# Four edits to a two-block transformer kernel: consumers of GpSimd powers, 128-row gate products, moved weights, an earlier final norm

## The chip, the cores and the metric

The kernel runs on one core of a Trainium2 chip, in one launch. Its time is the device time of that core in microseconds (us). Before the change the median of three runs is 1242.46 us (1242.16 to 1245.07). The profile is one further execution of 1242.75 us.

The engines are TensorE (PE in the profile; its weight loads are PEld), VectorE (DVE), ScalarE (ACT), GpSimd (POOL) and SyncE (SP), which issues most of the weight DMAs. Each engine works through its own queue in order, and waits there until what its next instruction reads is ready.

## The reference

Two transformer blocks follow each other on 512 tokens of width 1024, in fp32. Cut to what the change touches:

```python
# block 1
xn = rmsnorm(h, norm_mix_g)
q, k, v, u_vg, f = split(xn @ w_in)                 # 8 heads of 64
c = cumsum(log_sigmoid(f + b_forget))               # the gates, one column a head
att = softmax(causal(q @ k.T * scale + c_q - c_k)) @ v
u, vg = split(gelu(u_vg))
vg = rmsnorm(vg by groups of 64, v_gain)
h += concat(att, u * (tril(w_s) @ vg + b_s)) @ w_out
h += (silu(g) * a) @ w_down                         # a, g: conv3(rmsnorm(h) @ w_up)
x = rmsnorm(h, norm_final_g)
# block 2
h = modulate(rmsnorm(x), ...);  lat, krope, ca = split(h @ w_in_2)
o_ca  = chunk_attention(rmsnorm(ca_q), rmsnorm(ca_k), ca_v)      # 8 heads
o_mla = mla_attention(rope(rmsnorm(lat @ w_q_up)), ...)          # 8 heads
x += g_a * (concat(o_mla, o_ca) @ w_out_2)
x += g_m * ((silu(gate) * val) @ w_down_2)
```

## The kernel before

Activations lie in 128-partition tiles over the 512 tokens. An fp32 product is done as three products of rounded parts, high x high, high x low and low x high (`mm` in `gemm_fm`, `gemm_part`, `gemm_tm`, all recorded at L369). A weight piece arrives by DMA as `wraw`, ScalarE rounds it to `whi` (L347) and VectorE or GpSimd takes the rest as `wlo` (L348). Pieces are loaded ahead in the order of `make_plan`; the fourth entry of a plan item is a skew, in elements, of `whi` and `wlo` within their tiles of 1088 elements. Where `halves` is set a product runs over 256 tokens and then over the other 256: the first up tiles of the two FFNs, the last down tile, the latents, and the last parts of the attention outputs.

TensorE's order is the order of the code, written by hand. The orders of VectorE, ScalarE and GpSimd come from a scheduler that goes by readiness and priorities: `AHEAD` pulls the preparation of a head forward, `BEHIND` pushes background jobs back. A `Fill` is a list of generators that are run bit by bit between attention strips: `fill` holds products for TensorE, `bg` holds VectorE and GpSimd jobs such as normalisations and rope.

A strip is 128 queries of one head. `strip_scores` makes its scores on TensorE and the running minimum on VectorE (L590; the scores are negated), after which ScalarE makes the exponentials `p` (L594). One strip later `strip_turn` transposes `p` on TensorE (L603) and copies it to `pt` (L605), and after a further strip `strip_values` multiplies by the values into `o`. Block 1 has 32 strips, block 2 has 64; (h, q) is strip q of head h.

Inverse square roots are powers on GpSimd (L523) of a small tile: `ss` for the gated half of block 1 (used by VectorE at L1104 on `uv`), `ssc` for the queries and keys of the chunk attention (L1423 on `ca`), `nw` for the latent queries (L1514 on `mqk`). In block 1, `cumulate` puts the cumulated gates as high and low rows into `cum` (64 rows, L1213 and L1214), and for each head one product with a column of `pick` spreads them over 128 partitions (`mm<-cum,pick`); `ch` and `cm` are copied from it for the strip minima. The final norm of block 1 is `final`: a power, then per half of the tokens four products of `ms` with the identity (`to_rows`) and eight VectorE instructions on `x` (L912). Only the residual of block 2's output needs its result. It was put into `bg` when `mla(1)`, the second group of latent heads, was begun.

Of the kernel before, what the change touches and what calls it, by code (L numbers as in the profile page):

```python
# [2 lines left out]

# [7 lines left out]
F32 = mybir.dt.float32  # L11
# [222 lines left out]
class Kernel:  # L234
# [41 lines left out]
    def make_plan(self):  # L276
        i, plan = self.i, []

        def fm(name, tiles, kt0=0, nk=KT, pool=False, last=None):
            for n in tiles:  # L280
                for p in self.fm_pieces(i[name], n, kt0, nk):
                    plan.append((p, pool, None, 0))
            if last:
                plan[-1] = plan[-1][:2] + (last, 0)

        def tm(name, n, nk=KT, pool=True, last=None, per=None):
            skew = SKEW // 4 if n < 384 else 0
            for p in self.tm_pieces(i[name], n, nk, per):
                plan.append((p, pool, None, skew))
            if last:  # L290
                plan[-1] = plan[-1][:2] + (last, 0)

        def parts(name, dest):
            for p in range(4):
                for g in range(2):
                    plan.append((i[name][p, g], False, dest.get((p, g)), 0))

        def ffn(up, down, last=None):
            for j in range(NF):
                fm(up, [j, j + NF])  # L300
            fm(down, range(KT), 0, NF, last=last)

        tm("w_v", 512, pool=False, per=1)
        tm("w_g1", 264, pool=False)
        fm("w_qk", [0, 4])
        fm("w_qk", [1, 5])
        tm("w_g0", 256, pool=False)
        tm("w_u", 512)
        fm("w_qk", [2, 6], pool=True)
        fm("w_qk", [3, 7], pool=True)  # L310

        parts("w_out", {(3, 1): ("mx", "mix", "mix")})
        ffn("w_up", "w_down", ("cv", "cv", "cv"))
        fm("w_lat", range(3))
        tm("w_ck0", 256, pool=False, last=("one", "m0", "m1"))
        tm("w_cq0", 288, pool=False)
        tm("w_cv0", 256, pool=False)
# [12 lines left out]
        ffn("w_up_2", "w_down_2")  # L330
        self.plan, self.loaded, self.taken = plan, [], 0
        self.ada_left, self.pools, self.before = [], {}, []

    def load_split(self, src, pool, dest, skew):

# [179 lines left out]
    def rsqrt(self, x):  # L515
# [6 lines left out]
            e = e.rearrange("p (a b c) -> p a b c", b=shape[1], c=shape[2])  # L522
        self.nc.gpsimd.tensor_tensor(out=x, in0=x, in1=e, op=ALU.pow)  # L523

    def rstd(self, ms, scale, bias):

        r = self.sm.tile([P, 2], F32, tag="rstd", name="rstd", bufs=4)
        self.nc.vector.tensor_scalar(out=r, in0=ms, scalar1=scale, scalar2=bias, op0=ALU.mult, op1=ALU.add)
        self.rsqrt(r)
        return r  # L530
# [47 lines left out]
    def strip_scores(self, hd, qi):  # L578

        nc = self.nc  # L580
        nk = (qi + 1) * P
        n = max(nk, 256)
        s = self.bank("s")
        qk = hd["qk"]
        for j, (q, k) in enumerate(qk):
            self.mm(s[:, :n], q[:, qi * P:(qi + 1) * P], k[:, :n], j == 0, j == len(qk) - 1)
        st = self.sm.tile([P, 2], F32, tag="st", name="st", bufs=4)
        parts = hd["bias"](qi)
        for j, (cs, b) in enumerate(parts):
            nc.vector.tensor_tensor_reduce(  # L590
                out=s[:, cs], in0=s[:, cs], in1=b, scale=1.0, scalar=3e38 if j == 0 else st[:, j - 1:j],
                op0=ALU.add, op1=ALU.min, accum_out=st[:, j:j + 1])
# [410 lines left out]
    def block1_mix(self, xn, x, evac, evac_last, norm_a):  # L1003
# [24 lines left out]
        la = one.tile([P, 4, 8], F32, name="la")  # L1028


        cum = one.tile([64, 512], F32R, name="cum")
        pick = one.tile([64, 8], F32R, name="pick")
        nc.vector.tensor_tensor(out=pick, in0=self.ident[0:64, 0:8], in1=self.ident[0:64, 32:40], op=ALU.add)
        ss = one.tile([P, 2, 4, 4], F32, name="ss")


# [50 lines left out]
        def gate(j):  # L1087

            vs = [uv[t][:, 512 + 256 * j:768 + 256 * j] for t in range(4)]
            for t, v in enumerate(vs):  # L1090
                gelu2(v)
                sq = self.pp.tile([P, 512], F32, tag="p", name="sqg")[:, :256]
                nc.gpsimd.tensor_tensor(out=sq, in0=v, in1=v, op=ALU.mult)
                nc.vector.tensor_reduce(out=ss[:, j, t], in_=sq.rearrange("p (g d) -> p g d", d=64),
                                        axis=AX.X, op=ALU.add)
                yield 1200

            nc.vector.tensor_scalar(out=ss[:, j], in0=ss[:, j], scalar1=1.0 / 64, scalar2=4 * EPS,
                                    op0=ALU.mult, op1=ALU.add)
            self.rsqrt(ss[:, j])  # L1100
            yield 1500
            for t, v in enumerate(vs):
                v3 = v.rearrange("p (g d) -> p g d", d=64)
                nc.vector.tensor_tensor(out=v3, in0=v3, op=ALU.mult,  # L1104
                                        in1=ss[:, j, t].unsqueeze(2).to_broadcast([P, 4, 64]))
                nc.gpsimd.tensor_tensor(out=v, in0=v, in1=gg_row[:, 256 * j:256 * j + 256], op=ALU.mult)
                yield 700

# [36 lines left out]
        def qk(pr):  # L1145
            def ev(n, ps, cs):
                with self.tc.high_priority(offset=AHEAD):
                    if n < 4:
                        qf[pr] = two.tile([P, 512], F32, tag="qf", name="qf")
                        nc.vector.scalar_tensor_tensor(out=qf[pr], in0=ps, scalar=-0.125, in1=rrow,  # L1150
                                                       op0=ALU.mult, op1=ALU.mult)
                    else:
                        kf[pr] = two.tile([P, 512], F32, tag="kf", name="kf")
                        nc.vector.tensor_tensor(out=kf[pr], in0=ps, in1=rrow, op=ALU.mult)
            return self.gemm_fm(i["w_qk"], [pr, 4 + pr], xn, ev)

        def tm(w, dst):
# [48 lines left out]
        def cumulate():  # L1206

            cp = self.bank()[0:64]
            for t in range(4):
                for j, l in enumerate((lfh, lfl)):  # L1210
                    self.mm(cp[:, t * P:], l[:, t], tri[:, :512 - t * P], t == 0 and j == 0, t == 3 and j == 1)
            with self.tc.high_priority(offset=AHEAD):
                nc.scalar.copy(cum, cp)  # L1213
# [21 lines left out]
        def head(h):  # L1235
# [5 lines left out]
            def prepare(h):  # L1241
# [2 lines left out]
                qs = self.stack(stk, qf[pr], kf[pr], odd)  # L1244

                cp = self.bank()
                self.mm(cp, pick[:, h:h + 1].to_broadcast([64, P]), cum, True, True)
                ch = two.tile([P, 512], F32, tag="ch", name="ch")
                cm = two.tile([P, 512], F32, tag="cm", name="cm")
                nc.any.tensor_copy(out=ch, in_=cp)  # L1250
# [77 lines left out]

    def block2_mix(self, xn, norm_b, final, evac, evac_last, norm_a):
        nc, i = self.nc, self.i  # L1330
        ctx = ExitStack()
        self.pt = self.pool("pt2", 3, ctx=ctx)
        self.pp = self.pool("pp2", 3, ctx=ctx)
# [73 lines left out]
        def ca_norm(z, j):  # L1407
# [12 lines left out]
            yield 1500  # L1420
            for t in range(4):
                v3 = ca_slice(t, z, j).rearrange("p (g d) -> p g d", d=64)
                nc.vector.tensor_tensor(out=v3, in0=v3, op=ALU.mult,  # L1423
                                        in1=ss[:, j, z, t].unsqueeze(2).to_broadcast([P, 4, 64]))
                yield 400

        def cq0_evac(t, ps):
# [27 lines left out]
        def cq0():  # L1455
            yield from self.gemm_tm(i["w_cq0"], 288, xn, cq0_evac)
            bg.add("w_cq0", ca_norm(0, 0))
            bg.add("rope", rope())

        bg = Fill()  # L1460
        f = Fill([
# [42 lines left out]
        def q_norm(c):  # L1504
# [6 lines left out]
            for a in range(2):  # L1511
                v = mq[c][a]
                rq = r[:, 2 * a:2 * a + 2].unsqueeze(3)
                nc.vector.tensor_tensor(out=v, in0=v, in1=rq.to_broadcast([P, 2, 4, QK]), op=ALU.mult)  # L1514
# [34 lines left out]
        def mla(c):  # L1549
            if c == 0:  # L1550
                bg.add("kr", kr_rope())
            else:
                bg.add("final", final)
            mq[c] = m_tiles(0, c)
            yield from self.gemm_tm(i[f"w_q{c}"], 384, [lath[0], lath[1]], q_evac(c))
            bg.add(f"mq{c}", q_norm(c))
# [138 lines left out]
```

## Time and profile before

| | before |
|---|---|
| median of 3 runs | 1242.46 us |
| profiled execution | 1242.75 us |
| its span on the core | 1240.9 us |
| TensorE busy | 1206.9 us (97%) |
| VectorE busy | 792.5 us (64%) |
| ScalarE busy | 539.2 us (43%) |
| GpSimd busy | 194.2 us (16%) |
| mean granted clock of TensorE | 0.989 |

Of the 40 slices of the page, all but four have TensorE at 9 tenths or more; these four have 8, and three of them lie between 650 and 810 us, in the attention of block 2 (the fourth is the last). A busy TensorE may still run at half its clock or at a wider spacing than it could, so the start times of its products are read beside its busy time. In the timeline, what stands in brackets behind an instruction is how long its engine had been idle before it, and whose end released it.

### The profile page before, as it was taken

What the parts mean: (1) busy time and instruction counts of PE and PEld (TensorE: products, weight loads), DVE (VectorE), ACT (ScalarE), POOL (GpSimd) and SP (SyncE); (2) the same over time, 40 slices, a digit from 0 to 9 for tenths busy, and PEclk for the clock granted to TensorE, in tenths of its full rate; (3) what the DMA queues carried; (4) which work ended last, traced back from release to release, by engine and by line L of the source; (5) the groups of instructions that cost most, each with busy time, mean ns of one, the idle gap of its engine ahead of it and who ended that gap; (6) DMA issues with size and microseconds to landing.
All of it is one profiled execution on the core that took longest, in us unless ns stands there. A gap on an engine that the chain in (4) does not pass through costs nothing.

```text
span 1240.9 us, 17330 instructions
## 1 busy us (share of the span) xinstructions
PE 1206.9 (97%) x6730; PEld 1049.5 (85%) x6730; DVE 792.5 (64%) x1415; ACT 539.2 (43%) x963; POOL 194.2 (16%) x208
## 2 busy tenths in 40 slices
PE   9999999999999999999998998899999999999998
PEld 6887878988888888888998897789988888888887
DVE  6555877688888886433666779766676566553221
ACT  6444544444444443223435555664554444442110
POOL 1457400300000000000344452501200000000000
PEclk9999999999999999999999999999999999999999
DMA  7321212156666656433122111110132222233330
GB/s 242 99 86 48 73 68 69 52 190 200 189 202 195 193 185 193 129 94 114 56 103 64 56 69 61 51 35 18 69 119 87 101 102 92 96 94 103 117 110 17
DMA packets 40033, 131.57 MB, mean 106 GB/s; under 512 B 4608, under 2 KB 5504, under 8 KB 39952
## 3 DMA queue, kind: packets, MB, share of 16 engines
q1 hardware_dynamic: 31536, 102.64, 25.2%
q10 hardware_dynamic: 8208, 27.27, 7.1%
q8 instruction: 52, 0.85, 0.3%
q0 software_dynamic: 208, 0.57, 0.2%
q14 instruction: 29, 0.24, 0.1%
HBM read 128.37 MB, written 2.10 MB: 105 GB/s over the span
## 4 chain that ended last, share of the span: by engine, by line
PE 85%; DVE 7%; POOL 4%; ACT 2%; issue 2%; DMA 1%; SPq 0%; POOLq 0%; ACTq 0%; DVEq 0%
PE mm L369 74%; PE s L369 4%; PE o L369 3%; PE s L603 2%; DVE wlo L348 1%; DVE nt L550 1%; DMA x<-in_xT_dram 1%; DVE ca L1423 1%; DVE s L590 0%; POOL ss L523 0%; POOL nw L523 0%; PE s L695 0%; DVE kl L669 0%; DMA cs<-in_c_dram 0%; PE mm L1635 0%
## 5 line engine op out<-in xcount | busy, mean ns | idle before, releaser
L348 DVE TENSOR_TENSOR wlo<-wraw,whi 128x1024 fp32r<-128x1024 f32 (+4 forms) x182 | 210.4, 1158 | 182.0 <-ACT whi L347 181.2
L347 ACT CAST whi<-wraw 128x1024 fp32r<-128x1024 f32 (+4 forms) x194 | 192.2, 994 | 281.3 <-PE mm L369 261.8
L369 PE MATMUL mm<-xnh,whi 128*128 128x512 f32 (+1 forms) x832 | 312.4, 375 | 1.1 <-DVE nt L550 0.6
L369 PE MATMUL mm<-xnl,whi 128*128 128x512 f32 (+1 forms) x832 | 311.0, 374 | 0.0
L369 PE MATMUL mm<-xnh,wlo 128*128 128x512 f32 (+1 forms) x832 | 310.7, 373 | 0.0
L369 PEld LDWEIGHTS mm<-xnh,whi 128*128 128x128 f32 x832 | 157.0, 189 | 28.7 <-PE mm L369 0.8
L369 PEld LDWEIGHTS mm<-xnh,wlo 128*128 128x128 f32 x832 | 157.1, 189 | 27.7
L369 PEld LDWEIGHTS mm<-xnl,whi 128*128 128x128 f32 x832 | 157.2, 189 | 27.1
L369 PE MATMUL mm<-gh,whi 128*128 128x512 f32 (+1 forms) x384 | 141.6, 369 | 1.1 <-DVE x L937 0.6
L369 PE MATMUL mm<-gl,whi 128*128 128x512 f32 (+1 forms) x384 | 141.3, 368 | 0.0
L369 PE MATMUL mm<-gh,wlo 128*128 128x512 f32 (+1 forms) x384 | 141.3, 368 | 0.0
L729 DVE SCALAR_TENSOR_TENSOR cv<-mm,cols,cv 128x510 f32<-128x510 f32 (+1 forms) x176 | 130.4, 746 | 2.6 <-ACT cv L727 0.6
L369 PE MATMUL mm<-whi,xnh 128*128 128x256 f32 (+3 forms) x304 | 97.7, 321 | 0.2 <-ACT xnh L812 0.2
L369 PE MATMUL mm<-wlo,xnh 128*128 128x256 f32 (+3 forms) x304 | 94.3, 310 | 0.2 <-DVE wlo L348 0.2
L369 PE MATMUL mm<-whi,xnl 128*128 128x256 f32 (+3 forms) x304 | 94.2, 310 | 0.1
L369 PEld LDWEIGHTS mm<-gh,whi 128*128 128x128 f32 x384 | 72.4, 188 | 13.6 <-DVE x L937 0.8
L369 PEld LDWEIGHTS mm<-gl,whi 128*128 128x128 f32 x384 | 72.4, 188 | 12.1
L369 PEld LDWEIGHTS mm<-gh,wlo 128*128 128x128 f32 x384 | 72.4, 188 | 12.0
L594 ACT ACTIVATE p<-s,st 128x128 f32<-128x128 f32 (+1 forms) x96 | 50.7, 528 | 69.7 <-DVE st L590 66.7
L998 DVE CUSTOM_DVE_ANT_0 wada<-wada,cs,cols 128x1024 f32<-128x1024 f32 x48 | 61.5, 1282 | 26.9 <-DMA wada<-in_w_ada_dram 26.7
L369 PE MATMUL mm<-mix,whi 128*128 128x256 f32 (+1 forms) x288 | 74.4, 346 | 2.7 <-ACT vm L1563 1.2
L727 ACT ACTIVATE cv<-mm,cols 128x512 f32<-128x512 f32 x88 | 67.6, 772 | 0.2 <-PE mm L369 0.2
(293 smaller groups left out, 1839.1 us busy)
## 6 DMA issues: line engine op xcount, KB each, us to landing
wraw<-in_w_up_dram SPq DMA_DIRECT2D x88, 512.0 KB, 3.4
wada<-in_w_ada_dram ACTq DMA_DIRECT2D x48, 512.0 KB, 3.6
wraw<-in_w_down_dram SPq DMA_DIRECT2D x32, 512.0 KB, 3.5
wraw<-in_w_out_dram SPq DMA_DIRECT2D x16, 512.0 KB, 3.4
wraw<-in_w_down_dram SPq DMA_DIRECT2D x16, 384.0 KB, 3.1
wraw<-in_w_qk_dram SPq DMA_DIRECT2D x8, 512.0 KB, 3.7
wraw<-in_w_v_dram SPq DMA_DIRECT2D x8, 256.0 KB, 4.9
x<-in_xT_dram SPq DMA_DIRECT2D x8, 256.0 KB, 6.4
```

What stands on the lines that cost most here:

```text
L347: nc.scalar.copy(hi[:, :n], raw[:, :n])
L348: (nc.gpsimd if pool else nc.vector).tensor_tensor(out=lo[:, :n], in0=raw[:, :n], in1=hi[:, :n].bitcast(F32), op=ALU.subtract)
L369: self.nc.tensor.matmul(out, lhsT, rhs, start=start, stop=stop, **kw)
L550: self.applied = nc.vector.scalar_tensor_tensor(out=t, in0=x[k][:, cs], scalar=gain(k), in1=r, op0=ALU.mult, op1=ALU.mult).ins
L594: nc.scalar.activation(out=p[:, :nk], in_=s[:, :nk], func=AF.Exp, bias=st[:, len(parts) - 1:len(parts)], scale=-1.0, accum_out=hd["sums"](qi))
L603: self.nc.tensor.transpose(s[:, c], p[:, c], self.ident)
L727: nc.scalar.activation(out=t, in_=ps, func=AF.Identity, scale=w[2], bias=self.col(cb, n))
L729: nc.vector.scalar_tensor_tensor(out=t[:, d:], in0=ps[:, :512 - d], scalar=w[2 - d], in1=t[:, d:], op0=ALU.mult, op1=ALU.add)
L998: nc.vector.tensor_tensor_reduce(out=w, in0=w, in1=self.cs, scale=1.0, scalar=self.col("b_ada_2", n), op0=ALU.mult, op1=ALU.add, accum_out ...
L1423: nc.vector.tensor_tensor(out=v3, in0=v3, op=ALU.mult, in1=ss[:, j, z, t].unsqueeze(2).to_broadcast([P, 4, 64]))
```

## The change

1. Powers' consumers. `self.urgent` keeps the latest strip minimum (or, in block 1, the latest `kf` eviction). `late()` makes the instructions under it be placed behind that one on VectorE. It is put around the `uv`, `ca` and `mqk` multiplies with a power's result.
2. Gates. `cum` and `pick` get 128 rows, the lower half of `cum` is set to zero, and the product of each head has 128 rows.
3. Weights. Pieces of products that run in halves get a skew of `SKEW // 4` = 48 elements, 192 bytes. Pieces that are split into `wsplit` tiles keep theirs.
4. Final norm. `final` is added to `bg` right behind `rope`, in place of the beginning of `mla(1)`.

```diff
-        def fm(name, tiles, kt0=0, nk=KT, pool=False, last=None):
+        def fm(name, tiles, kt0=0, nk=KT, pool=False, last=None, skewed=()):
...
-                    plan.append((p, pool, None, 0))
+                    plan.append((p, pool, None, SKEW // 4 if n in skewed else 0))
...
-                    plan.append((i[name][p, g], False, dest.get((p, g)), 0))
+                    plan.append((i[name][p, g], False, dest.get((p, g)), SKEW // 4 if p in skewed else 0))
...
-                fm(up, [j, j + NF])
-            fm(down, range(KT), 0, NF, last=last)
+                fm(up, [j, j + NF], skewed=(0, 1, NF, NF + 1))
+            fm(down, range(KT), 0, NF, last=last, skewed=(KT - 1,))
...
-        parts("w_out", {(3, 1): ("mx", "mix", "mix")})
+        parts("w_out", {(3, 1): ("mx", "mix", "mix")}, (2, 3))
...
-        fm("w_lat", range(3))
+        fm("w_lat", range(3), skewed=range(3))
...
+    def late(self):
+
+        return self.tc.issue_after(self.urgent) if self.urgent else nullcontext()
...
-            nc.vector.tensor_tensor_reduce(
+            self.urgent = nc.vector.tensor_tensor_reduce(
...
-        cum = one.tile([64, 512], F32R, name="cum")
-        pick = one.tile([64, 8], F32R, name="pick")
-        nc.vector.tensor_tensor(out=pick, in0=self.ident[0:64, 0:8], in1=self.ident[0:64, 32:40], op=ALU.add)
+        cum = one.tile([P, 512], F32R, name="cum")
+        pick = one.tile([P, 8], F32R, name="pick")
+        nc.vector.tensor_tensor(out=pick, in0=self.ident[:, 0:8], in1=self.ident[:, 32:40], op=ALU.add)
+        nc.gpsimd.memset(cum[64:128].bitcast(F32), 0.0)
...
-                nc.vector.tensor_tensor(out=v3, in0=v3, op=ALU.mult,
-                                        in1=ss[:, j, t].unsqueeze(2).to_broadcast([P, 4, 64]))
+                with self.late():
+                    nc.vector.tensor_tensor(out=v3, in0=v3, op=ALU.mult,
+                                            in1=ss[:, j, t].unsqueeze(2).to_broadcast([P, 4, 64]))
...
-                self.mm(cp, pick[:, h:h + 1].to_broadcast([64, P]), cum, True, True)
+                self.mm(cp, pick[:, h:h + 1].to_broadcast([P, P]), cum, True, True)
...
             bg.add("rope", rope())
+            bg.add("final", final)
...
             if c == 0:
                 bg.add("kr", kr_rope())
-            else:
-                bg.add("final", final)
```

VectorE's order at the second normalisation of `uv` in block 1 (113 us) was, before; `ss` is what goes to the power, the `ISA` rows are the strip minima of `s` with `cm` or `ch`:

```order
L1098 TENSOR_SCALAR ss<-ss 128x16
L685 RECIPROCAL sums<-sums 128x8
L1104 TENSOR_TENSOR uv<-uv,ss 128x256 x3
L590 ISA s,st<-s,cm 128x128
L590 ISA st 128x1
L1104 TENSOR_TENSOR uv<-uv,ss 128x256
L590 ISA s,st<-s,cm 128x128
```

and is, in the changed kernel:

```order
L1103 TENSOR_SCALAR ss<-ss 128x16
L689 RECIPROCAL sums<-sums 128x8
L594 ISA s,st<-s,cm 128x128
L594 ISA st 128x1
L1110 TENSOR_TENSOR uv<-uv,ss 128x256
L594 ISA s,st<-s,cm 128x128
L594 ISA st 128x1
L594 ISA s,st<-s,ch,st 128x128
L594 ISA st 128x1
L1110 TENSOR_TENSOR uv<-uv,ss 128x256 x2
```

The first strip's minimum stands ahead of the first multiply, and the second strip's two ahead of the next two.

VectorE's order where block 2's attention begins (the stretch from 680 us), in the changed kernel; the `x_...` rows are the final norm, `wlo` and `bs` are a weight split and a bias strip:

```order
L594 ISA s,st<-s,bs 128x512
L594 ISA st 128x1
L916 SCALAR_TENSOR_TENSOR x_83<-x_83,cols,mm 128x256
L916 SCALAR_TENSOR_TENSOR x_84<-x_84,cols,mm 128x256
L916 SCALAR_TENSOR_TENSOR x_85<-x_85,cols,mm 128x256
L916 SCALAR_TENSOR_TENSOR x_86<-x_86,cols,mm 128x256
L916 SCALAR_TENSOR_TENSOR x_87<-x_87,cols,mm 128x256
L348 TENSOR_TENSOR wlo<-wraw,whi 128x256
L916 SCALAR_TENSOR_TENSOR x_88<-x_88,cols,mm 128x256
L916 SCALAR_TENSOR_TENSOR x_89<-x_89,cols,mm 128x256
L1614 TENSOR_SCALAR bs<-bs 128x512
L594 ISA s,st<-s,bs 128x128
```

Eight such rows, one half of the tokens, begin behind strip (0, 3); the other eight stand between strips (1, 1) and (1, 3). Before, all sixteen stood in one piece at 753 us. On TensorE the eight small products for them move with them, as two groups of four.

VectorE's order at the first latent queries (724 us), `nw` being what goes to the power, was, before:

```order
L1508 TENSOR_SCALAR nw<-nw 128x16
L1514 TENSOR_TENSOR mqk<-mqk,nw 128x768
L590 ISA s,st<-s,bs 128x384
L590 ISA st 128x1
L1514 TENSOR_TENSOR mqk<-mqk,nw 128x768
```

and is, in the changed kernel:

```order
L1517 TENSOR_SCALAR nw<-nw 128x16
L594 ISA s,st<-s,bs 128x384
L594 ISA st 128x1
L1524 TENSOR_TENSOR mqk<-mqk,nw 128x768
L673 TENSOR_TENSOR kl<-kf,kh 64x512
L594 ISA s,st<-s,bs 128x512
L594 ISA st 128x1
L673 TENSOR_TENSOR kl<-kf,kh 64x512
L1524 TENSOR_TENSOR mqk<-mqk,nw 128x768
```

One strip minimum moves ahead of each of the two multiplies.

## Rows read from the trace of the kernel before

**Rows 1.** The page: the chain that ended last, by engine.
```profile
PE 85%; DVE 7%; POOL 4%; ACT 2%; issue 2%; DMA 1%; SPq 0%; POOLq 0%; ACTq 0%; DVEq 0%
```

**Rows 2.** Busy time by stretches: `us, PE PEld DVE ACT POOL, PEclk, DMA, GB/s`.
```profile
275.00:300.00 25.00, 25.00 (x112) 20.71 (x111) 21.05 (x30) 10.02 (x14) 0.00 (x0) 1.00 0.62 195
...
675.00:700.00 25.00, 25.00 (x208) 24.79 (x207) 18.89 (x46) 13.49 (x34) 9.51 (x11) 1.00 0.27 80
```

**Rows 3.** Waits: `engine, line, waited for: us, times, longest`.
```profile
DVE ca L1423 <- POOL ssc L523: 11.1, 4, 3.0
```

**Rows 4.** Timeline at 113 us: `start, us, engine, line, operation [idle before <-releaser]`.
```profile
113.06 1.62 DVE L1104 TENSOR_TENSOR uv<-uv,ss 128x256 f32<-128x256 f32 x3 [2.92 <-POOL ss L523]
...
114.61 0.29 DVE L590 CUSTOM_DVE_ANT_0 s<-s,cm 128x128 f32<-128x128 f32 x1
...
115.57 0.33 PE L603 MATMUL s<-ident,p 128*128 128x128 f32 x1 [2.90 <-ACT p L594]
```

**Rows 5.** Busy time and granted clock (PEclk) in the stretch behind it.
```profile
115.95:119.30 3.35, 3.35 (x13) 2.82 (x11) 1.08 (x3) 3.14 (x7) 3.35 (x4) 0.50 0.02 5
```

**Rows 6.** Timeline at 62 us.
```profile
59.82 0.76 DVE L1104 TENSOR_TENSOR uv<-uv,ss 128x256 f32<-128x256 f32 x2 [3.02 <-POOL ss L523]
...
64.22 0.50 PE L369 MATMUL mm<-cum,pick 64*128 64x512 f32 x1 [2.04 <-DVE cum L1214]
```

**Rows 7.** Timeline at 703 and 724 us.
```profile
702.61 1.09 DVE L1423 TENSOR_TENSOR ca<-ca,ssc 128x256 f32<-128x256 f32 x3 [3.01 <-POOL ssc L523]
...
704.36 0.66 PE L695 MATMUL s<-ident,att 128*128 128x128 f32 x4 [1.53 <-DVE att L687]
...
705.97 0.50 PE L369 MATMUL s<-kh,qs 128*128 128x512 f32 x1 [0.78 <-DVE pt L605]
...
723.52 0.96 DVE L1514 TENSOR_TENSOR mqk<-mqk,nw 128x768 f32<-128x768 f32 x1 [3.03 <-POOL nw L523]
...
725.83 0.55 PE L603 MATMUL s<-ident,p 128*128 128x128 f32 x3 [2.46 <-ACT p L594]
```

**Rows 8.** Timeline at 741 us: a power on GpSimd, a split on VectorE.
```profile
741.14 2.91 POOL L523 TENSOR_TENSOR nw<-nw,nhalf 128x16 f32<-128x16 f32 x1 [6.52 <-DVE nw L1536]
...
742.89 1.22 DVE L348 TENSOR_TENSOR wlo<-wraw,whi 128x1024 fp32r<-128x1024 f32 x1
```

**Rows 9.** Timeline at 753 and at 780 us.
```profile
753.02 6.35 DVE L912 SCALAR_TENSOR_TENSOR x<-x,cols,mm 128x256 f32<-128x256 f32 x16 [0.23 <-PE mm L369]
...
755.03 0.74 PE L369 MATMUL mm<-mix,whi 128*128 128x512 f32 x2 [1.20 <-ACT vm L1563]
...
780.59 0.55 PE L603 MATMUL s<-ident,p 128*128 128x128 f32 x3 [1.40 <-ACT p L594]
...
785.56 0.33 PE L603 MATMUL s<-ident,p 128*128 128x128 f32 x1 [1.32 <-ACT p L594]
```

**Rows 10.** Timeline of TensorE at 139 us, around one product of the gates.
```profile
138.80 0.49 PE L369 MATMUL mm<-cum,pick 64*128 64x512 f32 x1
...
139.22 0.45 PE L369 MATMUL s<-kh,qs 128*128 128x384 f32 x1
...
139.69 0.39 PE L369 MATMUL mm<-xnh,whi 128*128 128x512 f32 x1
...
139.91 0.39 PE L369 MATMUL mm<-xnl,whi 128*128 128x512 f32 x1
```

**Rows 11.** Timeline of TensorE at 860 us, in the output product of block 2.
```profile
860.00 0.39 PE L369 MATMUL mm<-mix,whi 128*128 128x256 f32 x2
...
860.68 0.88 PE L369 MATMUL mm<-mix,wsplit 128*128 128x256 f32 x6
861.40 0.39 PE L369 MATMUL mm<-mix,whi 128*128 128x256 f32 x2
```

**Rows 12.** Half-width products by shape: `xcount | busy us, mean ns | idle`.
```profile
L369 PE MATMUL mm<-xnh,whi 128*128 128x256 f32 x128 | 36.7, 287 | 1.1 <-DVE nt L550 0.6 <-DVE x L847 0.5
...
L369 PE MATMUL mm<-gh,whi 128*128 128x256 f32 x76 | 21.8, 286 | 1.1 <-DVE x L937 0.6 <-DVE x L847 0.5
```

More of the change, by code (lines that the diff above doesn't have):

```diff
@@ L1 @@
-from contextlib import ExitStack
+from contextlib import ExitStack, nullcontext
 from itertools import chain
@@ L291, in tm, with parts @@
                 plan[-1] = plan[-1][:2] + (last, 0)
-        def parts(name, dest):
+        def parts(name, dest, skewed=()):
             for p in range(4):
                 for g in range(2):
-                    plan.append((i[name][p, g], False, dest.get((p, g)), 0))
+                    plan.append((i[name][p, g], False, dest.get((p, g)), SKEW // 4 if p in skewed else 0))
         def ffn(up, down, last=None):
             for j in range(NF):
-                fm(up, [j, j + NF])
-            fm(down, range(KT), 0, NF, last=last)
+                fm(up, [j, j + NF], skewed=(0, 1, NF, NF + 1))
+            fm(down, range(KT), 0, NF, last=last, skewed=(KT - 1,))
         tm("w_v", 512, pool=False, per=1)
@@ L331, in make_plan @@
         self.plan, self.loaded, self.taken = plan, [], 0
-        self.ada_left, self.pools, self.before = [], {}, []
+        self.ada_left, self.pools, self.before, self.urgent = [], {}, [], None
     def load_split(self, src, pool, dest, skew):
@@ L589, in strip_scores @@
         for j, (cs, b) in enumerate(parts):
-            nc.vector.tensor_tensor_reduce(
+            self.urgent = nc.vector.tensor_tensor_reduce(
                 out=s[:, cs], in0=s[:, cs], in1=b, scale=1.0, scalar=3e38 if j == 0 else st[:, j - 1:j],
-                op0=ALU.add, op1=ALU.min, accum_out=st[:, j:j + 1])
+                op0=ALU.add, op1=ALU.min, accum_out=st[:, j:j + 1]).ins
         p = self.pp.tile([P, 512], F32, tag="p", name="p")
@@ L1153, in ev @@
                         kf[pr] = two.tile([P, 512], F32, tag="kf", name="kf")
-                        nc.vector.tensor_tensor(out=kf[pr], in0=ps, in1=rrow, op=ALU.mult)
+                        self.urgent = nc.vector.tensor_tensor(out=kf[pr], in0=ps, in1=rrow, op=ALU.mult).ins
             return self.gemm_fm(i["w_qk"], [pr, 4 + pr], xn, ev)
@@ L1212, in cumulate @@
             with self.tc.high_priority(offset=AHEAD):
-                nc.scalar.copy(cum, cp)
+                nc.scalar.copy(cum[0:64], cp)
                 nc.vector.tensor_tensor(out=cum[32:64], in0=cp[32:64], in1=cum[32:64].bitcast(F32),
@@ L1330, in block2_mix @@
         nc, i = self.nc, self.i
+        self.urgent = None
         ctx = ExitStack()
@@ L1422, in ca_norm @@
                 v3 = ca_slice(t, z, j).rearrange("p (g d) -> p g d", d=64)
-                nc.vector.tensor_tensor(out=v3, in0=v3, op=ALU.mult,
-                                        in1=ss[:, j, z, t].unsqueeze(2).to_broadcast([P, 4, 64]))
+                with self.late():
+                    nc.vector.tensor_tensor(out=v3, in0=v3, op=ALU.mult,
+                                            in1=ss[:, j, z, t].unsqueeze(2).to_broadcast([P, 4, 64]))
                 yield 400
@@ L1513, in q_norm @@
                 rq = r[:, 2 * a:2 * a + 2].unsqueeze(3)
-                nc.vector.tensor_tensor(out=v, in0=v, in1=rq.to_broadcast([P, 2, 4, QK]), op=ALU.mult)
+                with self.late():
+                    nc.vector.tensor_tensor(out=v, in0=v, in1=rq.to_broadcast([P, 2, 4, QK]), op=ALU.mult)
                 rt = self.pp.tile([P, 4, 2, 4, 16], F32, tag="p", name="rt")
```

## The prediction

> **What bounds the kernel now.** I read four views in this order. The chain of waits comes first: TensorE holds 85% of it, VectorE 7% and GpSimd 4% [rows 1]. So TensorE decides, and the other two count where TensorE stands behind them. The busy time by stretches comes next: an FFN stretch has TensorE busy for 25.00 of 25 us, and so has 675 to 700; VectorE is at 18.89 us there, 6.11 us short of full [rows 2]. What is to be won lies in two things, therefore: places where TensorE stands, and products that could run at a smaller spacing. The list of waits names one cause of the standing: VectorE waits 11.1 us in four waits for GpSimd's powers at the normalisation of `ca` [rows 3]. Last I read the timeline around each such wait, and after it the granted clock.
>
> The pattern is plainest at 113 us. A `uv` multiply has stood 2.92 us for the power; the strip minimum queued behind it starts at 114.61, the exponential can't start before it, and the transposes at 115.57 have kept TensorE idle for 2.90 us [rows 4]. After it TensorE's granted clock is 0.50, its 1.2 GHz level, for 3.35 us [rows 5]; work done in that time would have taken half of it at 2.4 GHz, so the pause costs a further 1.7 us. Three other such pauses are followed by a stretch of the same length and clock (at 62, 702 and 724 us).
>
> **The change part by part.** Durations are those of the profiled execution, 1242.75 us with a span of 1240.9; the median of the runs shown is 0.3 us below it.
>
> *Consumers behind minima.* Four pauses hang on a power, and the new order puts minima (at the first also the `kf` eviction) ahead of its consumer.
> - At 62 us: the `uv` pair has waited 3.02 us, with `kf`, the stacking and `cum` queued behind it, and TensorE waits 2.04 us for `cum` [rows 6]. Worth 2.04 + 1.7 = 3.7.
> - At 113 us: 2.90 + 1.7 = 4.6 [rows 4, 5].
> - At 702 us: three `ca` multiplies stand behind a power for 3.01; `att` is behind them, TensorE waits 1.53 for it, and again 0.78 for a `pt` copy that is late in the same queue [rows 7]. 1.53 + 0.78 + 1.7 = 4.0.
> - At 724 us: `mqk`, then the minimum, then the transposes 2.46 late [rows 7]. 2.46 + 1.7 = 4.2.
>
> The sum is 16.5. The added waits, each for one minimum, cost nothing by themselves: a minimum runs within the same queue. Behind the waiting multiply stand the next strip's minimum and the `pt` copies; they suffer only if the power isn't there by then, which is the first rival. GpSimd's second multiply of `uv` comes later, as its VectorE partner does; its results go into the spatial products, which follow later in TensorE's order. SP's queue is as before.
>
> The multiplies now run while GpSimd is at other work, and a page speaks against that. In the trace a VectorE `wlo` subtraction with two SBUF operands starts at 742.89, in the middle of a power that spans 741.14 to 744.05, and takes 1.22 us, to 744.11 [rows 8]: it was not held to the power's end. The Trainium skill, "SBUF — State Buffer", section "SBUF: two separate sides", says that a VectorE instruction with two SBUF inputs and a GpSimd one that reads SBUF exclude each other for the whole instruction. By that rule every such instruction placed beside a power would be held for up to the rest of it, and the moved multiplies would give back up to 2.9 us at each of the four places; the row disagrees, so I give the rule no term.
>
> *The final norm next to rope.* Its sixteen VectorE instructions take 6.35 us at 753.02, amid the first products of the output, which wait 1.20 us for a `vm` copy [rows 9]. They go to the strips of the first two heads of block 2. Later strips are late as well, with another `mqk` among their minima: 1.40 us at 780.59 and 1.32 us at 785.56 [rows 9]. With 6.35 us less VectorE work ahead of them and `mqk` behind minima, these three are 3.9 us at most; the strip's own chain (minimum, exponential) remains, so I take two thirds, 2.6. The bound below is 6.35 us lost, if nothing around the new place covers it; above it is 3.9. The cover at the new place is the 6.11 us that VectorE has free in 675 to 700, almost exactly the 6.35 that come in.
>
> *128 rows for the gates.* The 64-row product at 138.80 holds the next start until 139.22, 0.42 us, where a 512-column product with 128 rows is followed after 0.22 us (139.69 to 139.91) [rows 10]. With 128 rows it should be like the others: 8 x 0.20 = 1.6 us, one product per head of block 1. Bounds: nothing, if the pause belongs to the operands' broadcast, and 8 x 0.42 = 3.4, if the other side of the product carries a like pause that the start times don't show. The fill of the lower half is one GpSimd write long before its first use.
>
> *Weights moved by 192 bytes.* Two runs of half-width products of one shape stand side by side in block 2's output: the six that start from 860.00 to 860.68 (the first two are one row) go at 0.68 / 6 = 0.113 us, the six from 860.68 to 861.40, with weights from the tiles `wsplit`, at 0.72 / 6 = 0.120 [rows 11]. By the addresses that the code gives, in the slower run the streamed operand lies at a multiple of 256 bytes from the next stationary one, in the faster run 64 bytes beside it, and 192 bytes is what the change adds in front of weights that now lie at such a multiple. The moved ones are, by the code, 3 x 128 products of the FFNs' first up tiles and 3 x 76 of the last down tiles [rows 12], 144 of the latents and 144 of block 1's output: 900. At 0.0067 us that is 6.0. Nothing in these rows is slower than 0.120, so the lower bound is 0. Some of the 900 stand where TensorE waits anyway, and the last pieces aren't moved: I take 0.7 of it, 4.2.
>
> *What comes back.* TensorE now arrives earlier at strips whose chain hasn't become shorter. I charge three waits of the size of the 1.32 us at 785.56, which left no second loss: 4.0.
>
> The sum: 16.5 + 2.6 + 1.6 + 4.2 - 4.0 = 20.9, so 1242.75 - 20.9 = 1221.8, and 1221.5 against the median. I write 1222.
>
> **The rivals.**
> 1. *The wait moves by a strip.* A consumer is held behind the latest minimum only; if the power ends later than that, the following minimum stands in the same way. For it: a power is 2.9 us long [rows 8], and at 113 us the new order has only one minimum ahead of the first multiply. Against it: the minimum was ready, it only stood in the queue, so TensorE's work of a whole strip now lies between. If it happens at 113 and 724 us, 4.6 + 4.2 come back: 1222 + 9 = 1231.
> 2. *The moved weights give nothing*, the spacing being set by the kind of product. For it: the slower six of rows 11 are also of another tile, so place and kind can't be told apart there. Then 1222 + 4 = 1226. The Trainium skill, "TensorE: Matmul & The Clock Gate", Part 2, step by step, would have it so: TensorE reads the streamed operand and the next weights through two independent ports, and loading doesn't take bandwidth from a running product. By that rule the six and the six should be equal; 0.120 against 0.113 in this trace speak against it.
> 3. *Slower: VectorE becomes the bound at the start of block 2.* 18.89 + 6.35 = 25.24 us is more than the stretch of 25 holds. If the final norm's instructions get ahead of minima there, VectorE is late by up to 6.35 us at the hand-over to each of the next three heads, each time with 1.7 us of halved clock: 3 x (6.35 + 1.7) = 24.2. The pauses at 702 and 724 then stay, too, and the change is left with 3.7 + 4.6 + 2.6 + 1.6 + 4.2 = 16.7: 1242.75 + 7.5 = 1250. It decides from a lateness of 16.7 / 3 - 1.7 = 3.9 us at each of the three. Against it: in the new order a minimum stands after every five to eight of those instructions, so one minimum meets 2 to 3.2 us of them, and a background job can wait.
>
> **How the numbers follow.** My forecast has 0.62, the moved wait 0.19 (with one of the two places, or another, in between), moved weights without effect 0.11, VectorE as the bound 0.05, and 0.03 goes to a loss in between that leaves less than 0.3% (3.7 us, about what a measurement tells from no change). The forecast's own range is 1213 to 1229: at the best end all bounds at once, 16.5 + 3.9 + 3.4 + 6.0 = 29.8. The range to hold the time 8 times in 10 takes in the moved wait and part of a worse placing of the final norm: 1212 to 1235. Faster by over 0.3%: 0.91; within: 0.04; slower: 0.05.
>
> **What would show it.** Right: no idle TensorE at `cum` (62 us), at 113, 702 and 724 us, and no clock of 0.50 behind them; the `cum` product followed after 0.22; the FFN's first tiles at a spacing of 0.113; the sixteen instructions beside a TensorE that is busy throughout. Wrong: VectorE waits of 2 us or more for a power with a minimum right behind; idle TensorE between 675 and 700; the spacing at 0.120 still. The prediction as a whole is wrong if the four pauses stay or new ones with a halved clock come up in block 2's first heads.

## The result, and the profile after

The changed kernel takes 1231.31 us (median of four runs, 1229.92 to 1234.45) against 1243.76 for the one before on the same chip: a ratio of 0.9899 (95% interval 0.9879 to 0.992). Measured again it is 1230.75 us, 0.9885 (0.9867 to 0.9902). So it is 12 to 14 us faster; 20.9 were forecast. The profiled execution is 1232.63 us with a span of 1230.9; both are 10 us below the profile of before.

Chain of waits, page of the kernel after:

```profile
PE 85%; DVE 6%; POOL 4%; ACT 2%; issue 2%; DMA 1%; SPq 0%; ACTq 0%; POOLq 0%; DVEq 0%
```

Busy time of the two stretches that answer to [rows 2], each moved by what the kernel is ahead there, and the waits for powers on VectorE:

```profile
265.20:290.20 25.00, 25.00 (x112) 20.71 (x111) 20.10 (x29) 9.97 (x14) 0.00 (x0) 1.00 0.61 185
...
665.00:690.00 25.00, 25.00 (x211) 24.78 (x209) 22.85 (x58) 15.07 (x38) 8.58 (x10) 1.00 0.26 80
```

```profile
DVE ca L1431 <- POOL ssc L523: 5.9, 2, 3.0
```

The `ca` line has two waits of 5.9 us in all where there were four of 11.1 [rows 3], one wait of 2.7 us is left for `uv` (of 5.9) and one of 2.4 for `mqk` (of 4.3), each behind the minimum that it stood in front of. VectorE now stands at 22.85 us in the stretch that had 18.89, and TensorE is at 25.00 there still. The first pause is gone: in the timeline at 62 us the product of the gates starts without any idle time before it, where it had 2.04 us [rows 6].

```profile
62.27 0.40 PE L369 MATMUL mm<-cum,pick 128*128 128x512 f32 x1
```

At 113 us the pause has changed its place. Timeline of the kernel after, GpSimd, VectorE and TensorE:

```profile
107.85 0.27 PE L607 MATMUL s<-ident,p 128*128 128x128 f32 x1
...
108.72 2.38 POOL L348 TENSOR_TENSOR wlo<-wraw,whi 128x1024 fp32r<-128x1024 f32 x1
108.79 2.58 DVE L1110 TENSOR_TENSOR uv<-uv,ss 128x256 f32<-128x256 f32 x1 [2.67 <-POOL ss L523]
...
111.96 3.07 DVE L1110 TENSOR_TENSOR uv<-uv,ss 128x256 f32<-128x256 f32 x2
...
112.16 2.58 POOL L348 TENSOR_TENSOR wlo<-wraw,whi 128x1024 fp32r<-128x1024 f32 x1
...
116.25 2.35 POOL L348 TENSOR_TENSOR wlo<-wraw,whi 128x1024 fp32r<-128x1024 f32 x1
...
116.43 0.63 PE L699 MATMUL s<-ident,att 128*128 128x128 f32 x4 [1.80 <-DVE att L691]
...
116.99 1.89 DVE L1110 TENSOR_TENSOR uv<-uv,ss 128x256 f32<-128x256 f32 x1
...
118.21 0.50 PE L369 MATMUL s<-kh,qs 128*128 128x512 f32 x1 [0.99 <-ACT pt L609]
```

The transposes that had waited 2.90 us [rows 4] start at 107.85 with no wait. But a single `uv` multiply takes 2.58 us at 108.79, two take 3.07, and one 1.89; two took 0.76 at 59.82 [rows 6]. Each of these three lies beside a GpSimd `wlo` split of 2.4 to 2.6 us and ends 0.3 us behind it. What stands behind them on VectorE, `att`, comes late: TensorE waits 1.80 and then 0.99 us. Its clock did not fall this time, while behind the waits at 700 and 720 us, told next, it did:

```profile
116.00:119.40 3.40, 1.98 (x11) 1.70 (x12) 3.14 (x7) 1.42 (x4) 3.40 (x3) 1.00 0.36 129
700.60:703.90 3.30, 3.30 (x18) 3.30 (x17) 2.26 (x6) 2.76 (x6) 1.12 (x3) 0.50 0.80 300
720.90:724.30 3.40, 3.40 (x16) 3.40 (x15) 2.84 (x8) 1.93 (x5) 1.37 (x3) 0.53 0.48 159
```

The two places in block 2 in the timeline of the kernel after:

```profile
693.68 0.60 PE L699 MATMUL s<-ident,att 128*128 128x128 f32 x4
...
700.24 0.75 PE L1604 MATMUL mm<-ident,ca 128*128 128x128 f32 x4 [1.98 <-DVE mqk L1500]
```

```profile
713.11 0.49 PE L607 MATMUL s<-ident,p 128*128 128x128 f32 x3
...
720.23 0.37 ACT L598 ACTIVATE p<-s,st 128x128 f32<-128x128 f32 x1 [4.02 <-DVE nw L1510]
...
720.74 0.33 PE L607 MATMUL s<-ident,p 128*128 128x128 f32 x1 [1.62 <-ACT p L598]
```

The waits of 1.53, 0.78 and 2.46 us [rows 7] are gone: `att` at 693.68 and the transposes at 713.11 follow without idle time. In their stead the second four key transposes wait 1.98 us for a `mqk` evacuation (0.33 before), and the transposes of the next strip 1.62 us for an exponential. Of the 1.20 us for `vm` [rows 9] 0.99 are left at 743.42, for a `mqk` evacuation.

Where the time was won can be read by comparing the start of each TensorE product with that of the same product before. By the times of the trace of before, the changed kernel is 0.3 us behind at 61 us and ahead by 3.9 at 70, 4.7 at 112, 6.5 at 128, 9.8 at 270, behind block 1's attention, and 10.0 at the end. (Some 1.7 of the 9.8 is a stretch of 3.4 us at the lower clock at 177 us, which before has and this execution hasn't.) So in this execution block 2's attention gave back all that it won. In the profile of the second measurement (span 1227.3 us) it is 9.7 at 270 us and 13.6 at the end. Most of the difference lies behind a wait of 2.89 us, at 738 us in the one and 737 in the other, that the kernel before has too (749.28): the clock then stays at its lower level for 10.2 us in the first execution and for 3.4 in the second. The first execution, then the second:

```profile
738.10:748.30 10.20, 8.98 (x31) 7.50 (x32) 5.43 (x11) 5.30 (x15) 0.00 (x0) 0.50 0.32 103
```

```profile
737.50:740.90 3.40, 3.40 (x17) 3.22 (x16) 1.86 (x4) 2.72 (x6) 0.00 (x0) 0.50 0.47 153
741.00:747.30 6.30, 5.30 (x29) 4.33 (x29) 5.17 (x10) 2.98 (x9) 0.73 (x1) 1.00 0.25 86
```

The products of the gates in the kernel after; the row behind 139.22 [rows 10] in the trace of before; and the half-width products of the kernel after:

```profile
110.15 0.48 PE L369 MATMUL mm<-cum,pick 128*128 128x512 f32 x1
110.46 0.33 PE L369 MATMUL s<-kh,qs 128*128 128x384 f32 x1
110.63 0.34 PE L369 MATMUL s<-kl,qs 128*128 128x384 f32 x1
```

```profile
139.50 0.34 PE L369 MATMUL s<-kl,qs 128*128 128x384 f32 x1
```

```profile
865.00 0.28 PE L369 MATMUL mm<-xnh,whi 128*128 128x256 f32 x1
...
869.00 0.28 PE L369 MATMUL mm<-xnl,whi 128*128 128x256 f32 x1
```

The next start behind the 128-row product is 0.31 us away, not the 0.42 of before, and that behind it 0.17, not 0.28; the value product ahead of it starts 0.08 us before it, not 0.21. From 865.00 to 869.00 there are 34 half-width products of the FFN at 0.1177 us each: less than 0.120, but not the 0.113 of [rows 11].

### The profile page after: what moved, and what is told of

Same layout as the page of the kernel before. It is cut to its first block, busy times and chain, and to the rows that moved or that the text cites. A ratio compares the mean times of both kernels' runs of the same rounds, so it can differ in the third digit from the quotient of the medians.

```text
span 1230.9 us, 17327 instructions
## 1 busy us (share of the span) xinstructions
PE 1198.8 (97%) x6730; PEld 1044.5 (85%) x6730; DVE 799.9 (65%) x1414; ACT 539.2 (44%) x964; POOL 194.3 (16%) x209
## 4 chain that ended last, share of the span: by engine, by line
PE 85%; DVE 6%; POOL 4%; ACT 2%; issue 2%; DMA 1%; SPq 0%; ACTq 0%; POOLq 0%; DVEq 0%
PE mm L369 75%; PE s L369 4%; PE o L369 3%; PE s L607 2%; POOL wlo L348 1%; DVE wlo L348 1%; DVE ca L1431 1%; DVE s L594 1%; DMA x<-in_xT_dram 1%; DVE nt L554 1%; ACT p L598 1%; PE mm L1643 0%; ACT whi L347 0%; DVE kl L673 0%; PE s L699 0%
## 5 line engine op out<-in xcount | busy, mean ns | idle before, releaser
L369 PEld LDWEIGHTS mm<-gh,whi 128*128 128x128 f32 x384 | 72.1, 188 | 13.6 <-DVE x L941 0.8
```

Source lines behind the costliest of these rows:

```text
L369: self.nc.tensor.matmul(out, lhsT, rhs, start=start, stop=stop, **kw)
```

## The experiments

In each, the ratio is against the kernel before on the same chip, over all runs of both; times gained on the kernel before are worked out from it, and can differ by 0.8 us from the difference of the two medians. The first four are the four parts alone, on the kernel before.

**Consumers behind minima alone.**

```diff
+                with self.late():
                     nc.vector.tensor_tensor(out=v3, in0=v3, op=ALU.mult,
...
```

> Only part 1, the consumers of powers behind minima. The prediction: 16.5 us less and up to 4.0 given back, so 12.5 to 16.5 us faster than before. The theory from the trace after: the uv and ca multiplies now stand beside GpSimd's weight splits and ahead of evacuations, so two of the four places give most back; 5 to 8 us faster, with a new TensorE wait of 1.5 us or more at the att transposes near 116 us and one near 700 us.

Measured 1235.45 us, 0.9926 (0.9903 to 0.9949): 9.2 us faster (6.3 to 12.1), between the two expectations; the interval reaches into the second. The waits near 116 us are in this trace too, at 1.07 and 0.99 us, and so is the one near 700, 1.98 us at 703.50.

**The final norm alone.**

```diff
             bg.add("rope", rope())
+            bg.add("final", final)
...
-            else:
-                bg.add("final", final)
```

> Only part 4, the final norm next to rope. The prediction: 2.6 us faster (bounds 3.9 faster, 6.35 slower). The theory from the trace after: 0, within 1.5 us, since what it frees at 753 us is taken again by waits up to 790 us.

Measured 1247.21 us, 1.0026 (1.001 to 1.0041): 3.2 us slower (1.2 to 5.1). Both expectations miss; the lower bound of the prediction (6.35 slower) holds it. VectorE and TensorE in the timeline of this kernel:

```profile
685.81 2.83 DVE L912 SCALAR_TENSOR_TENSOR x<-x,cols,mm 128x256 f32<-128x256 f32 x7
...
688.55 0.56 DVE L590 CUSTOM_DVE_ANT_0 s<-s,bs 128x384 f32<-128x384 f32 x1
...
694.02 0.43 DVE L1423 TENSOR_TENSOR ca<-ca,ssc 128x256 f32<-128x256 f32 x1 [2.59 <-POOL ssc L523]
...
695.20 0.70 DVE L590 CUSTOM_DVE_ANT_0 s<-s,bs 128x512 f32<-128x512 f32 x1
...
696.87 0.66 PE L603 MATMUL s<-ident,p 128*128 128x128 f32 x4 [1.10 <-ACT p L594]
...
708.08 0.66 PE L695 MATMUL s<-ident,att 128*128 128x128 f32 x4 [2.31 <-DVE att L687]
```

Seven of the sixteen stand in front of a minimum (2.83 us). VectorE is then late for the `ca` normalisation: its power starts at 691.09, where it started at 680.14 before. The multiply waits 2.59 us for it in front of the next minimum, and TensorE gets a new wait of 1.10 us; the one for `att` grows from 1.53 to 2.31.

**The weights alone.**

```diff
-                fm(up, [j, j + NF])
-            fm(down, range(KT), 0, NF, last=last)
+                fm(up, [j, j + NF], skewed=(0, 1, NF, NF + 1))
+            fm(down, range(KT), 0, NF, last=last, skewed=(KT - 1,))
...
```

> Only part 3, the weights moved by 192 bytes. The prediction: 4.2 us faster (0 to 6.0), spacing 0.113 us. The theory from the trace after: spacing 0.1175 in place of 0.120 for about 870 products, 2.1 us faster. The rival that place does nothing: 0.

Measured 1244.1 us, 0.9998 (0.9984 to 1.0011): 0.2 us faster, between 2.0 faster and 1.4 slower. The spacing is what the trace after has: 34 products from 876.29 to 880.30 in the timeline of this kernel. At 0.0023 us for each of some 870 products that is 2.0 us, at the edge of the interval. Zero is not excluded either. And place alone doesn't give the 0.113: in the profiled execution of the changed kernel 18 products of block 1's first up tiles go at 0.1135 us (226.32 to 228.25), in the second profile of that same kernel the same 18 at 0.1176 (226.39 to 228.39).

**The gates alone.**

```diff
-        cum = one.tile([64, 512], F32R, name="cum")
+        cum = one.tile([P, 512], F32R, name="cum")
...
-                self.mm(cp, pick[:, h:h + 1].to_broadcast([64, P]), cum, True, True)
+                self.mm(cp, pick[:, h:h + 1].to_broadcast([P, P]), cum, True, True)
```

> Only part 2, 128 rows for the gates. The prediction: 1.6 us faster (0 to 3.4). The theory from the trace after: from the start of the last value product ahead of it to the second product behind it each of the eight takes 0.34 us less, 2.5 us in all.

Measured 1239.91 us, 0.9962 (0.9945 to 0.9978): 4.7 us faster (2.7 to 6.8). That is above the prediction's bounds in the middle, and its lower end is the 2.7 us that eight times 0.34 make. Where more than that would come from isn't shown; the clock can do it. The profiled execution is the slowest of the twelve, and in it TensorE's products gain 4.2 us between 50 and 270 us: the 2.7, and what was lost in a stretch of 3.4 us at the lower clock at 177 us that the trace of before has and this one hasn't. It loses them again to stretches at the lower clock, 6.8 us at 602 us, where before had 3.4, and 3.4 at 786, where before had none.

The four alone sum to 9.2 - 3.2 + 0.2 + 4.7 = 10.9 us, and together they give 12 to 14.

**The changed kernel again**, beside the next three.

> The changed kernel itself, beside the three that are made from it. 12.5 us faster than before, if the sum of its four parts run alone holds (9.2 + 4.7 + 0.2 - 3.2 = 10.9) 11 us.

Measured 1230.75 us, 0.9885, as told above.

**The splits beside the `uv` multiplies on VectorE.**

```diff
-        fm("w_qk", [2, 6], pool=True)
-        fm("w_qk", [3, 7], pool=True)
+        fm("w_qk", [2, 6])
+        fm("w_qk", [3, 7])
```

> The changed kernel with the low parts of the query and key weights of pairs 2 and 3 (four splits, between 103 and 119 us) on VectorE in place of GpSimd. Theory that the late uv multiplies are held by these splits: each uv multiply takes 0.4 to 0.5 us in place of 2.58, 1.5 and 1.89, the TensorE waits of 1.80 and 0.99 us at 116 to 118 us shrink to under 1 us in sum, and the kernel is 1.5 to 3.5 us faster than the changed one. Rival, that the pause only moved with the end of the power: the multiplies are fast, but the waits stay, and it is no faster. A second rival: VectorE, with 4 x 1.2 us more, makes TensorE wait more; 2 us slower.

Measured 1227.86 us, 0.987 (0.9851 to 0.9889): 2.9 us below the changed kernel by medians, with intervals that overlap. VectorE and TensorE in its timeline:

```profile
107.58 0.43 DVE L1110 TENSOR_TENSOR uv<-uv,ss 128x256 f32<-128x256 f32 x1 [2.53 <-POOL ss L523]
...
110.85 0.76 DVE L1110 TENSOR_TENSOR uv<-uv,ss 128x256 f32<-128x256 f32 x2
...
114.40 0.60 PE L699 MATMUL s<-ident,att 128*128 128x128 f32 x4
...
115.58 0.42 DVE L1110 TENSOR_TENSOR uv<-uv,ss 128x256 f32<-128x256 f32 x1
```

The multiplies are at 0.43, 0.76 for two, and 0.42, and the transposes of `att` start without a wait; the 0.99 us behind them are gone as well. The power was waited for as before (2.53 us). So the splits held the multiplies, and those held `att`. The second rival falls too: VectorE had room for four splits.

The splits held the power back as well. In the trace of before the scaling of `ss` that the power reads takes 2.27 us beside a split, where the same instruction took 0.17 at 56.63; the power began behind it at 110.12, by an estimate from these two durations 2.1 us later than it could. TensorE's pause there was 2.90 us [rows 4]. In this run it takes 0.17 again, and the power begins at 103.66, in place of 105.84. It then takes 3.89 us, not 2.91: a VectorE split had started 0.06 us ahead of it. Two rows of before, then two of this run:

```profile
107.50 2.51 POOL L348 TENSOR_TENSOR wlo<-wraw,whi 128x1024 fp32r<-128x1024 f32 x1 [2.93 <-ACT whi L347]
107.77 2.27 DVE L1098 TENSOR_SCALAR ss<-ss 128x16 f32<-128x16 f32 x1
```

```profile
103.60 1.18 DVE L348 TENSOR_TENSOR wlo<-wraw,whi 128x1024 fp32r<-128x1024 f32 x1
103.66 3.89 POOL L523 TENSOR_TENSOR ss<-ss,nhalf 128x16 f32<-128x16 f32 x1 [3.46 <-DVE ss L1103]
```

So `att`, 3.4 us earlier on VectorE than in the changed kernel (112.19 for 115.61), owes 1.2 us of that to the earlier end of the power and the rest to the multiplies.

**The final norm put back** in the changed kernel, the reverse of the second edit.

> The changed kernel with the final norm put back to the beginning of the second group of latent heads. The prediction (2.6 us won by moving it): 2.6 us slower than the changed kernel. From the part run alone (3.2 us lost by moving it): 3.2 us faster, about 1228.

Measured 1232.03 us, 0.9896 (0.9877 to 0.9915): 1.3 us above the changed kernel by medians, which the intervals don't tell from nothing. The move that costs 3.2 us alone costs nothing to be seen beside the other parts. One reason is that the multiply that waited 2.59 us in front of a minimum stands behind it there: the run without late `ca` multiplies, below, has that wait of TensorE back (1.11 us for 1.10).

**Four buffers for `p`.**

```diff
-        self.pp = self.pool("pp2", 3, ctx=ctx)
+        self.pp = self.pool("pp2", 4, ctx=ctx)
```

> The changed kernel with four instead of three buffers for p in block 2 (rope's temporaries and the squares use them too). Theory that the exponential of strip (4, 0), which ended 4.02 us of idle ScalarE behind a reduction of nw, waits for such a buffer: TensorE's wait of 1.62 us at 720.7 us goes to under 0.8 us, and 1 to 3 us are won. Rival, that its minimum behind rope's multiplies sets it: the wait and the time stay as in the changed kernel.

Measured 1231.07 us, 0.9886 (0.9864 to 0.9908), the same as the changed kernel; the 1 to 3 us aren't seen, though an interval of +-3 us doesn't exclude 1. The wait of 1.62 us is gone, so it was for the buffer, but a next one is there for `att`:

```profile
719.94 0.27 PE L607 MATMUL s<-ident,p 128*128 128x128 f32 x1
...
725.58 0.63 PE L699 MATMUL s<-ident,att 128*128 128x128 f32 x4 [1.11 <-DVE att L691]
```

**The `ca` multiplies not late** in the changed kernel.

```diff
-                with self.late():
-                    nc.vector.tensor_tensor(out=v3, in0=v3, op=ALU.mult,
-                                            in1=ss[:, j, z, t].unsqueeze(2).to_broadcast([P, 4, 64]))
+                nc.vector.tensor_tensor(out=v3, in0=v3, op=ALU.mult,
+                                        in1=ss[:, j, z, t].unsqueeze(2).to_broadcast([P, 4, 64]))
```

> The changed kernel without part 1 for the ca multiplies alone (uv and mqk stay behind minima). The prediction's size (4.0 us at 702 us won by it): 4.0 us slower than the changed kernel, about 1235. From the trace after, where 4.1 us won up to the second key transposes are followed by 1.98 us of waiting and 0.8 us of halved clock there: 1.2 us slower, within 2 us either way.

Measured 1234.72 us, 0.9925 (0.9906 to 0.9944): 4.0 us above the changed kernel by medians, the prediction's size. The two weren't measured side by side; by their ratios to the kernel before it is 3.2 to 5.0. My reading of the trace after had counted too little: without `late` the pause for `att` is back, at 2.31 us, and with the final norm in its new place a wait of 1.11 us at 687 comes with it. So the agreement with 4.0 is luck in part: the prediction's terms were 1.53 and 0.78 us of waiting and 1.7 of halved clock, while here the two waits are those of the final norm alone (1.10 and 2.31).

```profile
687.26 0.66 PE L607 MATMUL s<-ident,p 128*128 128x128 f32 x4 [1.11 <-ACT p L598]
...
696.71 1.09 DVE L1430 TENSOR_TENSOR ca<-ca,ssc 128x256 f32<-128x256 f32 x3 [3.01 <-POOL ssc L523]
...
698.46 0.90 PE L699 MATMUL s<-ident,att 128*128 128x128 f32 x3 [2.31 <-DVE att L691]
```

**Splits and buffers together**, and the same without late `ca` multiplies.

> The changed kernel with the four splits on VectorE and with four buffers for p in block 2, both of the earlier ones together. If each removes its wait and they don't meet: the 1.80 and 0.99 us at 116 us and the 1.62 us at 720 us are gone, 3 to 5 us faster than the changed kernel, about 1227. If such waits only pass on to the next place: no faster than the one with the splits alone, 1228 to 1230.

> The same with the ca multiplies not behind minima. The prediction's size: 4.0 us slower than the kernel with both. If at 700 us nothing is won by the order, since the transposes behind wait for a bank that VectorE frees late: within 1.5 us of it.

Measured 1228.51 us, 0.9879 (0.9859 to 0.99), no faster than the splits alone: the buffer's wait passes on. Without late `ca` it is 1233.45 us, 0.9915 (0.9898 to 0.9932), 4.9 us more, measured side by side: the second theory falls, and the same two waits are there (1.11 and 2.32).

**The keys' normalisation on VectorE** as well, behind minima. At 735 us the trace after has the same pattern as at 113, at a place that the change doesn't touch, with the 2.89 us of TensorE that the kernel before has at 749.28; that was the second longest in its two attentions, and the prediction had no term for it. GpSimd and VectorE:

```profile
733.18 1.20 POOL L1552 TENSOR_TENSOR mqk<-mqk,nw 128x512 f32<-128x512 f32 x1
733.52 1.41 DVE L670 TENSOR_TENSOR qs<-qf,qs 64x512 fp32r<-64x512 f32 x1
...
734.94 2.46 DVE L673 TENSOR_TENSOR kl<-kf,kh 64x512 fp32r<-64x512 f32 x2
735.37 1.49 POOL L1552 TENSOR_TENSOR mqk<-mqk,nw 128x512 f32<-128x512 f32 x1
...
738.32 0.48 PE L607 MATMUL s<-ident,p 128*128 128x128 f32 x1 [2.89 <-ACT p L598]
```

```diff
-                nc.gpsimd.tensor_tensor(out=v[:, :, :, 0:64], in0=v[:, :, :, 0:64],
-                                        in1=rk.to_broadcast([P, 2, 4, 64]), op=ALU.mult)
+                with self.late():
+                    nc.vector.tensor_tensor(out=v[:, :, :, 0:64], in0=v[:, :, :, 0:64],
+                                            in1=rk.to_broadcast([P, 2, 4, 64]), op=ALU.mult)
...
```

(and the same for the rope part of the keys, on the kernel with the splits on VectorE)

> The changed kernel with the four splits on VectorE, and with the four multiplies that normalise the latent keys (735 us, GpSimd) on VectorE behind strip minima as well. If GpSimd's two-operand work holds VectorE there (qs 1.41 for 0.69 us, two kl 2.46 for 1.38), the TensorE wait of 2.89 us at 738 us and the halved clock behind it shrink by 1.5 to 4.5 us: about 1225. Rival, that VectorE's load there sets the minimum: the multiplies only change the engine, and the time stays at 1228.

Measured 1223.97 us, 0.9829 (0.9812 to 0.9846), 3.9 us below the kernel with the splits alone (5 by the ratios, as the two weren't measured side by side). This version beats both kernels, the changed one by 6.8 us in the medians, with intervals that don't touch. In its timeline two `kl` take 1.38 us where they took 2.46, the multiplies take 0.68 and 0.42 on VectorE, where GpSimd took 1.20 to 1.49 and 1.06, and the wait is 1.39 us in place of 2.89, with no stretch at the lower clock behind it:

```profile
727.63 1.38 DVE L673 TENSOR_TENSOR kl<-kf,kh 64x512 fp32r<-64x512 f32 x2
...
730.25 0.33 PE L607 MATMUL s<-ident,p 128*128 128x128 f32 x1 [1.39 <-ACT p L598]
...
730.73 0.68 DVE L1553 TENSOR_TENSOR mqk<-mqk,nw 128x512 f32<-128x512 f32 x1
731.33 0.42 DVE L1556 TENSOR_TENSOR mqk<-krr,nw 128x256 f32<-128x256 f32 x1
```

## Why the prediction was right or wrong

The direction and the main cause were right, and the time lies in the range; the size was off by 7 to 9 us, and the first rival's 1231 is what came. That number is luck in part: the places were right (113 and 724 us), but no following minimum stood for the power, as the rival has it; the gain was lost to GpSimd's splits at the one and to a buffer at the other, and other terms were off both ways. In block 2 the prediction fails by its own sign: new pauses came up in the first heads, 1.98 and 1.62 us, with a clock of 0.50 and 0.53 behind them.

- *Consumers behind minima, 16.5 less what comes back.* Right at 62 us, where the pause is gone and nothing took its place: 4.1 us were won between 61 and 70 us, 3.7 were forecast. At 702 us the order counts (4.0 us lost when undone, 4.9 in the kernel with splits and buffers), though the trace alone wouldn't show it and part of that size belongs to the final norm's new place. At 113 us the step failed that gave VectorE and GpSimd holding each other off no term, by one row [rows 8]: it took the power for GpSimd's work in general. A power in its middle did not hold VectorE; the splits that GpSimd runs right behind it did, and the late multiplies meet these. The trace of before had a row for it, the `ss` scaling of 2.27 us. Of 2.90 us 2.79 came back, without the halved clock in this execution: 1.9 us were won between 112 and 128 us, 4.6 were forecast. The experiment with the splits shows why. At 724 us the wait went to the next strip, 1.62 us, by a buffer that rope's and the squares' temporaries share with `p`, and when that was freed to the next `att`.
- *What comes back, 4.0.* Mis-sized: three short waits were charged, and the places above have 1.80 + 0.99 + 1.98 + 1.62 = 6.4 us (0.33 of it was there before), with a halved clock behind the one at 700 and again at 721 us.
- *The final norm, 2.6 won.* Wrong in sign by itself: 3.2 us slower. The cover that I named, the 6.11 us that VectorE has free in 675 to 700, is free there in sum, but not in front of the minimum that the seven instructions meet. Beside the late multiplies it costs nothing to be seen. What it was to free is free in part: of the 3.9 us of [rows 9] 1.6 are left in the changed kernel, beside 1.02 at 767.36 where 0.14 stood. That VectorE would become the bound (the third rival) didn't happen: 22.85 us of 25, with TensorE full.
- *The gates, 1.6.* Too small: the pause of the 64-row product lies on both sides, 0.11 us behind it, 0.11 behind the next product and 0.12 ahead, 0.34 in all and 2.7 us for eight.
- *The weights, 4.2.* Mis-sized: the spacing went to 0.1177 us, not 0.113, so 2.0 us by the trace, and alone 0.2 were measured. The faster six of [rows 11] had the right place and something else too that makes them fast; what, stays open, and it comes and goes between executions of one kernel. The second rival (nothing) isn't excluded by the time, but the spacing speaks against it.

Put together: 9.2 for the first part instead of 12.5, -3.2 to about 1 for the norm instead of 2.6, 2.7 to 4.7 for the gates instead of 1.6, 0.2 to 2.0 for the weights instead of 4.2.

## What to carry to other kernels

When an instruction is moved out of the way of a queue, look at what the other engine will run beside it in the new place, not only at what it leaves behind. A wait that is taken away at one strip can be charged again at the next resource of that strip (a buffer, an evacuation); only the sum over the next two or three strips is the gain. A part that loses by itself can be free beside another part that moves the waiting instruction behind the urgent one, so parts are tried together and alone.

## What the runs showed of the hardware

GpSimd's power (128x16, 2.91 us) didn't hold a VectorE split that began in its middle, but its splits and multiplies of two SBUF operands did: 2.58 us for one `uv` multiply that takes 0.43 beside none, 1.41 for a `qs` of 0.69, 2.46 for two `kl` of 0.69 each, and 2.27 for a scaling of `ss` (128x16, one tile) of 0.17. A power that began 0.06 us behind a VectorE split took 3.89 us. The Trainium skill, "SBUF — State Buffer", section "SBUF: two separate sides", says that such pairs exclude each other for the whole instruction; these rows agree, [rows 8] with the power does not. Why a power is held at its start and doesn't hold in its middle is open. A pause of 1.80 and 0.99 us left TensorE's granted clock at 1.00 (116.00 to 119.40), and 1.98 us were followed by 0.50. That is no rule for the length of a pause: in the run with four buffers the same two waits (1.78 and 0.99 us, at 116.39 and 118.17) are followed by the lower level, and behind one and the same wait of 2.89 us it lasted 10.2 and 3.4 us in two executions of one kernel.

```profile
117.90:121.30 3.40, 3.13 (x7) 2.49 (x8) 2.56 (x6) 0.70 (x2) 3.34 (x4) 0.50 0.40 152
```

A 64-row product among 128-row ones cost 0.34 us more than one padded with zeros; the Trainium skill, "TensorEngine Tiling (Array Packing)", section "Key Properties", has it that a change of the tiling mode drains TensorE, which these rows agree with.
